# Prologue of a two-layer encoder kernel: squares on other engines, one transposition earlier, three small loads on ScalarE's queue

## The chip, the cores and the metric

The kernel runs on one core of one Trainium2 chip. The metric is the device time of one execution in microseconds; three runs of the kernel before gave 933.13, 933.24 and 934.04 us, and their median, 933.24 us, is the time before. A core has a tensor engine (TensorE, PE in the profile; its weight loads are PEld), a vector engine (VectorE, DVE), a scalar engine (ScalarE, ACT), GpSimd (POOL) and SyncE (SP), which here only starts transfers. Transfers (DMAs) can be started from the queues of SyncE, ScalarE and GpSimd.

## The reference

A trunk of two layers works on 512 tokens of 1024 numbers, all float32. Layer 0 mixes by dilated window attention (three dilations, 8 heads of 128), layer 1 by grouped-query attention with rotary angles over a grid; both also attend to 256 memory tokens with 4 heads. Cut to what matters here:

```python
for i in range(DEPTH):                       # 2 layers
    h = rmsnorm(x, norm_g[i])                # x * rsqrt(mean(x*x) + EPS) * g
    mem_h = rmsnorm(mem, mem_norm_g[i])
    proj = einsum('bsd,de->bse', h, w_in)    # q, k, v of the mixer, memory queries, gate
    o_mix = mixer(...)                       # q and k normed per head (qn, kn), rotary, softmax, values
    o_mem = memory_attention(q_mem, mem_h, w_mem_kv[i], ...)
    y = concat([o_mix, o_mem]) * silu(gate)
    x = x + einsum('bse,ed->bsd', y, w_out[i])
```

The squares in this text are the `mean(x*x)` of the first two lines for layer 0. The "table" is the rotary table of layer 0 (`tab_a`), the "norm rows" are `qn_a` and `kn_a`, the first 32 gains of each.

## The kernel before

**Products.** Every float32 matmul is made of three: an operand is cut into a high part (a cast to the matmul type, on ScalarE) and a low part (what is left, a subtraction on VectorE). A matmul group computes high x high and low(activation) x high(weight) first (`mm_early`, L178 and L179), then high(activation) x low(weight) (`mm_late`, L182). Large products are done by a seven-product scheme over quarter matrices (`s_chunk`); the memory keys and values of layer 0 are plain products (`proj_t` through `chunk`).

**Weights.** `Weights` loads tiles `wl` of 512 KB by SyncE's queue (L260), adds some of them up (L291 on VectorE, L287 to L306 as adding transfers from GpSimd's queue), casts them to `wh` on ScalarE (L331, with a gain; L333) and subtracts to `wo` on VectorE (L345, L347). `advance` does this once for each group of matmuls: low parts, sums, high parts, loads.

**Order of the work.** The order on each engine is the order in which the Python program emits instructions. `Driver` keeps it: after each group of 8 early and 4 late matmuls comes a `tick`, a slot; generators that were spawned with a delay take a step when their slot has come, in the order in which they were spawned, and `yield n` asks for n slots. An engine works in order, so an instruction that waits holds up everything behind it on that engine. Each of the three DMA queues is in order in the same way.

**The prologue.** Slots 1 to 8 are the memory keys and values (two products of two halves `u` of the weights, each with two blocks `b` of 128 memory tokens); slots 9 to 22 are the first seven products of layer 0 on the tokens. Before the first group, SyncE issues the memory rows (`mt`, in four pieces of 256 KB), the first weights, four blocks of tokens (`xt`, 512 KB each) and the gains, interleaved. Then, line by line:

- `square(b, j)` (L1276 on ScalarE, L1278 on VectorE) takes the squares of a piece of memory rows; `factor(b)` makes from them the root of the mean on GpSimd (L1283, `rstd_of` L535 and L536).
- `place_m(b, j)` (L1288) transposes a piece on TensorE (`turn4`, L589: four transposes into one bank) and cuts it into high and low (`split`, L166 on ScalarE, L169 on VectorE). `place_m(1, 0)` makes the first half of block 1, the operand of the second group.
- `ahead(u, b)` (L1311) is what is put between the early and the late matmuls of the groups of the memory keys; `proj_t` (L606) calls it as `mid`. In slot 1, `(0, 0)`, that is: square of piece (1, 0) on ScalarE, `place_m(1, 0)`, square of piece (0, 1) on VectorE, and two high weight parts (L331).
- `norm_1(xb, both)` (L568) takes the squares of a token block: both halves on ScalarE (L576) for `both` 0, the second half on VectorE (L574) for 1, both halves on VectorE for 2; then three small GpSimd instructions (L578, L535, L536) make the root. `norm_2` (L583) scales the block by it on VectorE.
- `prep` (L1223) is the generator for the token blocks. Its slots 4, 5, 6 are `c` = 2, 3, 4. In slot 4 it takes the squares of blocks 2 and 3 (of block 2 one half on ScalarE and one on VectorE, of block 3 both on VectorE) and brings in block 0 (`first_t`, L644: eight transposes L589, two casts L166, two subtractions L169, two copies L650). In slot 5 it scales block 2 and brings in block 1; in slot 6 it scales block 3. From slot 7 on (`diffs_t`, `rest_t`) the sums and differences of the blocks are made.
- The evacuation of the memory keys (`ev_k`, L764) squares them per head on ScalarE (`head_sq`, L704, four instructions) and makes its root on GpSimd (L535, L536 with four columns, then L770).
- `setup` (L1253) is spawned for slot `SET_AT` = 15: it issues three loads on SyncE's queue, the rotary table (128 rows of 1024 bytes) and twice 3 x 32 gains to all 128 partitions (384 pieces of 128 bytes each), and four slots later (slot 19) begins the small computations with them on VectorE (L1259 to L1263), later the table itself (L1266).

```python
    drv.spawn(prep(), PD)            # PD = 2
    drv.spawn(setup(), SET_AT)       # 15
    ...
    km, vm = mem_kv(0, M, ahead)     # slots 1 to 8
    s_chunk(512, H, ev_v0, tight=True)   # slots 9 to 22
```

Of the kernel before, what the change touches and what calls it, by code (L numbers as in the profile page):

```python
# [21 lines left out]
TCKW = {}  # L22
NBIG, NM4, NS2, SCRATCH = 7, 23, 14, 2048
RING, LEAD = 4, 2
BULK, ACTIVE, SET_AT, MEM_B, PREP_Y, PREP_B, HALF, SET_B = 2, 2, 15, 14, 1, 1, {"a": 3, "b": 3, "o": 0}, 12
MEM_STEP = 1, 1
MEM_D = 4
PAUSE = 2
# [105 lines left out]
def trunk_kernel(ctx: ExitStack, tc: tile.TileContext, x, mem, wall, norm_g, mem_norm_g, gcol,  # L134
                 qn_a, kn_a, qn_b, kn_b, ident_d, mask_d, tab_a, tab_b, out):
    nc = tc.nc
# [15 lines left out]
    def s2(dt=F32, name="s2"):  # L152
        return pool.tile([128, 512], dt, tag="s2", name=name, bufs=NS2)
# [7 lines left out]
    def sm(n, name):  # L161
        return small.tile([128, n], F32, tag="sm%d" % n, name=name)
# [13 lines left out]
    def mm_early(o, a, b, c, d, start):  # L176

        T.matmul(o, a, b, start=start, stop=False, skip_group_check=True)  # L178
        T.matmul(o, c, d, start=False, stop=False, skip_group_check=True)  # L179

    def mm_late(o, a, b, stop):
        T.matmul(o, a, b, start=False, stop=stop, skip_group_check=True)  # L182
# [200 lines left out]
    def chunk(units, nb, group, evac):  # L383

        ps = [None] * nb
        for u in range(units):
            w = []
            for h, l in (W.take(), W.take()):
                w += [(h[:, k * 512:(k + 1) * 512], l[:, k * 512:(k + 1) * 512]) for k in range(2)]
            for b in range(nb):  # L390
                if u == 0:
                    ps[b] = pj()
                group(w, u, b, ps[b])
                drv.free()
                if u == units - 1:
                    drv.release(evac(b, ps[b]), 2)
                W.advance()
                drv.tick()
# [132 lines left out]
    def rstd_of(ss, n):  # L531

        r = sm(n, "rstd")
        e = sm(n, "mse")
        G.tensor_scalar(e, ss, EPS, None, ALU.add)  # L535
        G.tensor_tensor(r, e, half[:, 0:n], ALU.pow)  # L536
        return r
# [30 lines left out]
    def norm_1(xb, both=False):  # L568

        ss = sm(2, "ss")  # L570
        for j in range(2):
            jk = s2(name="sq")
            if both and (j or both == 2):
                V.tensor_tensor_reduce(jk, xb[j], xb[j], 1.0 / 1024.0, 0.0, ALU.mult, ALU.add, ss[:, j:j + 1])  # L574
            else:
                A.activation(jk, xb[j], AF.Square, scale=1.0 / 32.0, accum_out=ss[:, j:j + 1])  # L576
        r, e = sm(1, "rstd"), sm(1, "mse")
        G.tensor_tensor(e, ss[:, 0:1], ss[:, 1:2], ALU.add)  # L578
        return rstd_of(e, 1)

    def norm_2(xb, r, row, js=(0, 1)):
        for j in js:
            V.scalar_tensor_tensor(xb[j], xb[j], r, row[j], ALU.mult, ALU.mult)  # L583
# [22 lines left out]
    def proj_t(act, sels, evac, mid=None):  # L606

        def group(w, u, b, p):
            for k in range(4):
                kk = 4 * u + k  # L610
                mm_early(p, sels[b](act, 0, kk), w[k][0], sels[b](act, 1, kk), w[k][0], kk == 0)
            if mid:
                mid(u, b)
            for k in range(4):
                kk = 4 * u + k
                mm_late(p, sels[b](act, 0, kk), w[k][1], kk == 7)
        chunk(2, len(sels), group, evac)
# [26 lines left out]
    def first_t(H, top, c, view=same, turn=same):  # L644

        ps = [(k, turn(turn4(top[j], None, None)), [view(t) for t in slot(H, k, c)]) for k, j in (("12", 1), ("11", 0))]
        for k, p, hl in ps:
            split(*hl, p)
        for k, p, _ in ps:
            A.copy(view(whole(k, c)), p)  # L650

    def diffs_t(H, low, c, view=same, turn=same, late=False):

        f22 = whole("22", c)
        A.copy(view(f22), turn(turn4(low[1], None, None)))
        p = turn(turn4(low[0], None, None))
        yield 1
        s1, s3 = whole("S1", c), whole("S3", c)
        V.tensor_tensor(view(s1), p, view(f22), ALU.subtract)
        V.tensor_tensor(view(s3), view(full["11", c]), p, ALU.subtract)  # L660
        hl = slot(H, "S1", c)
        if late:
            drv.late(lambda: split(*hl, s1))
        else:
            split(*hl, s1)

    def rest_t(H, c, ds, spread=False):

        def put(k, f):
            hi, lo = slot(H, k, c)  # L670
            A.copy(hi, f)

            def low():
                V.tensor_tensor(lo, f, hi.bitcast(F32), ALU.subtract)
                yield 1

            if c and k == "S2" and not spread:
                drv.release(low(), 1)
            else:
                (drv.soon if spread and c and k == "S2" else drv.late)(lambda: next(low()))  # L680

        s1, s2_, s4, s3, f22 = [full.pop((k, c)) for k in ("S1", "11", "12", "S3", "22")]
        V.tensor_tensor(s2_, s1, s2_, ALU.subtract)
        if not spread:
            V.tensor_tensor(s4, s4, s2_, ALU.add)
        put("S2", s2_)
        if spread:
            yield ds[0] - 1
            V.tensor_tensor(s4, s4, s2_, ALU.add)
            yield 1  # L690
        else:
            yield ds[0]
        put("S4", s4)
        yield ds[1]
        put("S3", s3)
        yield ds[2]
        put("22", f22)
        yield 1
# [24 lines left out]
    def halves(t):  # L723
        return [t[:, 0:512], t[:, 512:1024]]
# [483 lines left out]
    tabA = s2(name="tabA")[:, 0:256].rearrange("p (b c d) -> p b c d", b=2, c=4)  # L1208
    grA = s2(name="grA")[:, 0:192].rearrange("p (s c) -> p s c", s=6)
# [9 lines left out]
    xb = [halves(t) for t in xt]  # L1219

    n = {}

    def prep():  # L1223

        for c in range(5):
            if c > 2:
                norm_2(xb[c - 1], n[c - 1], rows["x"])
            if c == 2:
                n[2], n[3] = norm_1(xb[2], 1), norm_1(xb[3], 2)
            if 1 < c < 4:  # L1230
                first_t(H, xb[c - 2], c - 2, by_class, from_rows)
            yield 1

        def forms(c):
            yield from diffs_t(H, xb[2 + c], c, by_class, from_rows, late=True)
            yield 3
            yield from rest_t(H, c, (2, 2, 2))

        drv.spawn(forms(1), 1)
        yield from forms(0)  # L1240
# [11 lines left out]

    def setup():  # L1253

        nc.sync.dma_start(tabA.rearrange("p b c d -> p (b c d)"), tab_a.rearrange("(a i) f -> i a f", i=4))
        nc.sync.dma_start(grA[:, 0:3], qn_a[0:1, :, 0:32].to_broadcast([128, 3, 32]))
        nc.sync.dma_start(grA[:, 3:6], kn_a[0:1, :, 0:32].to_broadcast([128, 3, 32]))
        yield 4
        V.tensor_tensor(gk, gc[:, 0:3], gc[:, 3:6], ALU.mult)  # L1259
        V.tensor_scalar(gk, gk, QS, None, ALU.mult)  # L1260
        V.tensor_scalar(gc[:, 6:8], gc[:, 6:8], QS, None, ALU.mult)
        V.memset(gk[0:32, :], 1.0)
        V.tensor_scalar(grA[:, 0:3], grA[:, 0:3], QS, None, ALU.mult)  # L1263
        yield 6
        for cs_ in range(2):
            V.tensor_tensor(ropeA[:, cs_], tabA[:, cs_, :, None, :].to_broadcast([128, 4, 6, 32]),  # L1266
                            grA[:, None].to_broadcast([128, 4, 6, 32]), ALU.mult)
            yield 1
# [4 lines left out]
    def square(b, j, act=True):  # L1273

        if act:
            A.activation(s2(name="sq"), mb[b][j], AF.Square, scale=1.0 / 32.0, accum_out=ss[b][:, j:j + 1])  # L1276
        else:
            V.tensor_tensor_reduce(s2(name="sq"), mb[b][j], mb[b][j], 1.0 / 1024.0, 0.0, ALU.mult, ALU.add, ss[b][:, j:j + 1])  # L1278
# [9 lines left out]
    def place_m(b, j, act=True):  # L1288

        p = turn4(mb[b][j], None, None)  # L1290
        split(*[M.block(n, j, slice(b * 128, (b + 1) * 128)) for n in range(2)], p, act)
# [19 lines left out]
    def ahead(u, b):  # L1311

        if (u, b) == (0, 0):
            square(1, 0)
            place_m(1, 0)
            square(0, 1, False)
            W.hi(True)
            W.hi(True)
        if (u, b) == (0, 1):
            place_m(0, 1)  # L1320
            factor(0)
            square(1, 1, False)
            place_m(1, 1)
            n[0] = norm_1(xb[0])
            n[1] = norm_1(xb[1])
            factor(1)
        if (u, b) == (1, 0):
            norm_2(xb[0], n[0], rows["x"])
            norm_2(xb[1], n[1], rows["x"])
# [660 lines left out]
```

## Time and profile before

| | |
|---|---|
| median of three runs | 933.24 us (933.13 to 934.04) |
| profiled execution, its own time | 933.17 us |
| span of its profile, first to last instruction | 931.4 us |
| TensorE busy | 924.8 us, 99% |
| weight loads of TensorE | 814.7 us, 87% |
| VectorE busy | 801.7 us, 86% |
| ScalarE busy | 695.7 us, 75% |
| GpSimd busy | 360.5 us, 39% |
| granted TensorE clock | 1.000 |

Rows of the timeline read: start in us, duration in us, engine, line, operation, output <- inputs, shapes, how many in a row; in brackets the time for which the engine stood before it and what ended that. A `q` behind an engine's name means its instruction sequencer, where DMAs are issued. Rows of the waits read: who waited, for whom, us in total, times, longest. Rows of the stretches read: from:to, length, then busy us and number of instructions for PE, PEld, DVE, ACT, POOL, then the granted clock, the busy share of the DMA engines and GB/s. Rows of the chain read: start, duration, what. A line number names the line of the kernel before, and of a helper where a helper emits the instruction.

### The profile page before, as it was taken

The numbers are of one execution on the slowest core, as the hardware profiler recorded it, in microseconds if no ns is written. First come the engines' busy times: TensorE is split into PE (matmuls) and PEld (weight loads), VectorE is DVE, ScalarE is ACT, GpSimd is POOL, SyncE is SP. The second block draws the span as 40 slices with busy tenths as digits, with TensorE's granted clock in tenths as the row PEclk, the third lists the DMA queues.
The fourth block names the chain that finished last, engine by engine and source line by source line (L and its number), as shares of the span: only waits on it lengthen the run. The fifth ranks groups of instructions, "written<-read, shape, count | busy, mean of one in ns | idle before, by whom it ended". The sixth has DMA issues, their size and how long they took to land.

```text
span 931.4 us, 16276 instructions
## 1 busy us (share of the span) xinstructions
PE 924.8 (99%) x5471; PEld 814.7 (87%) x5471; DVE 801.7 (86%) x1457; ACT 695.7 (75%) x1725; POOL 360.5 (39%) x504
## 2 busy tenths in 40 slices
PE   9999999999999999999999999999999999999998
PEld 7789888888888888888889998888988999999886
DVE  6999677879888888979798989999898998789977
ACT  7775789677868686867776767757879887789774
POOL 4411425556564646464746102234252440110122
PEclk9999999999999999999999999999999999999999
DMA  9999948968686778686867899999985687785777
GB/s 351 389 264 331 300 127 218 319 146 247 162 248 166 249 160 271 159 272 135 241 178 207 231 261 271 289 320 331 289 219 114 178 233 178 201 227 116 200 162 181
DMA packets 83179, 212.85 MB, mean 229 GB/s; under 512 B 18960, under 2 KB 25752, under 8 KB 83096
## 3 DMA queue, kind: packets, MB, share of 16 engines
q1 hardware_dynamic: 60744, 141.16, 42.3%
q0 software_dynamic: 20384, 67.12, 39.1%
q10 hardware_dynamic: 1968, 3.54, 1.0%
q8 instruction: 43, 0.70, 0.3%
q14 instruction: 40, 0.33, 0.1%
HBM read 162.96 MB, written 12.65 MB: 189 GB/s over the span
## 4 chain that ended last, share of the span: by engine, by line
PE 91%; DVE 5%; DMA 2%; ACT 1%; SPq 0%; issue 0%; DVEq 0%; ACTq 0%
PE pj L178 24%; PE pj L179 24%; PE pj L182 24%; PE qT L716 3%; PE sa L1476 2%; PE oo L1585 2%; PE ptb L1819 1%; PE sa L1472 1%; DVE wo L347 1%; PE pt L1564 1%; DMA x<-in_x_dram 1%; DMA row<-in_norm_g_dram 1%; PE ob L178 1%; PE ob L182 1%; PE ob L179 1%; PE xT L589 1%
## 5 line engine op out<-in xcount | busy, mean ns | idle before, releaser
L347 DVE TENSOR_TENSOR wo<-wl,wh 128x1024 fp32r<-128x1024 f32 x253 | 308.8, 1225 | 5.6 <-ACT wh L333 5.6
L333 ACT CAST wh<-wl 128x1024 fp32r<-128x1024 f32 x253 | 267.3, 1061 | 27.5 <-PE pj L179 19.5
L178 PE MATMUL pj<-wh,hS 128*128 128x512 f32 (+1 forms) x416 | 154.5, 380 | 0.0
L179 PE MATMUL pj<-wh,hS 128*128 128x512 f32 (+1 forms) x416 | 148.9, 367 | 0.0
L178 PE MATMUL pj<-wh,h 128*128 128x512 f32 (+1 forms) x312 | 115.3, 378 | 0.0
L179 PE MATMUL pj<-wh,h 128*128 128x512 f32 (+1 forms) x312 | 111.6, 367 | 0.0
L536 POOL TENSOR_TENSOR rstd<-mse,half 128x4 f32<-128x4 f32 (+2 forms) x98 | 102.0, 1041 | 8.2
L182 PE MATMUL pj<-wo,hS 128*128 128x512 f32 (+1 forms) x416 | 99.5, 366 | 0.0
L179 PEld LDWEIGHTS pj<-wh,hS 128*128 128x128 f32 x416 | 78.7, 189 | 11.2
L178 PEld LDWEIGHTS pj<-wh,hS 128*128 128x128 f32 x416 | 78.6, 189 | 11.0
L535 POOL TENSOR_SCALAR mse<-hss 128x4 f32<-128x4 f32 (+1 forms) x88 | 45.6, 519 | 104.4 <-ACT junk L704 91.3
L182 PEld LDWEIGHTS pj<-wo,hS 128*128 128x128 f32 x416 | 72.4, 189 | 13.0 <-DVE wo L347 0.2
L704 ACT ACTIVATE junk<-sn 128x128 f32<-128x128 f32 x264 | 79.3, 310 | 3.4 <-DVE sn L428 3.4
L260 POOL DMA_DIRECT2D wl<-in_wall_dram x44 | 41.9, 982 | 95.4 <-DMA wl<-in_wall_dram 21.7
L1417 POOL TENSOR_TENSOR ta<-sn,tabs 128x128 f32<-128x128 f32 (+1 forms) x64 | 38.3, 605 | 104.0 <-DVE sn L709 80.4
L415 ACT COPY sn<-pj 128x512 f32<-128x512 f32 x122 | 67.2, 590 | 12.3 <-PE pj L182 12.3
L182 PE MATMUL pj<-wo,h 128*128 128x512 f32 (+1 forms) x312 | 74.5, 366 | 0.0
L306 POOL DMA_DIRECT2D wl<-wl x35 | 31.0, 895 | 109.2 <-DVE wo L347 48.7
L438 DVE TENSOR_TENSOR sn<-pj,sn 128x512 f32<-128x512 f32 x89 | 60.7, 683 | 6.5 <-PE pj L182 6.2
L179 PEld LDWEIGHTS pj<-wh,h 128*128 128x128 f32 x312 | 59.0, 189 | 8.4
L178 PEld LDWEIGHTS pj<-wh,h 128*128 128x128 f32 x312 | 59.0, 189 | 8.2
L296 POOL DMA_DIRECT2D wl<-wl x35 | 32.9, 964 | 78.7 <-DVE wl L291 18.9
(299 smaller groups left out, 2403.0 us busy)
## 6 DMA issues: line engine op xcount, KB each, us to landing
wl<-in_wall_dram SPq DMA_DIRECT2D x226, 512.0 KB, 7.4
wl<-wl POOLq DMA_DIRECT2D x70, 512.0 KB, 5.9
wl<-in_wall_dram POOLq DMA_DIRECT2D x48, 512.0 KB, 8.6
od<-o SPq DMA_DIRECT2D x9, 256.0 KB, 5.8
x<-in_x_dram SPq DMA_DIRECT2D x4, 512.0 KB
v0r<-sn SPq DMA_DIRECT2D x8, 256.0 KB, 8.5
v0d<-v0r SPq DMA_DIRECT2D x4, 512.0 KB
og<-od ACTq DMA_DIRECT2D x4, 512.0 KB
```

What stands on the lines that cost most here:

```text
L178: T.matmul(o, a, b, start=start, stop=False, skip_group_check=True)
L179: T.matmul(o, c, d, start=False, stop=False, skip_group_check=True)
L182: T.matmul(o, a, b, start=False, stop=stop, skip_group_check=True)
L260: queue.dma_start(t, wall[d], **how)
L333: A.copy(wh, self.tile[key])
L347: V.tensor_tensor(wo, self.tile[key], wh.bitcast(F32), ALU.subtract)
L415: A.copy(t_, b_)
L438: V.tensor_tensor(t_, b_, t_, ALU.subtract if q == "12" and late is None else ALU.add)
L535: G.tensor_scalar(e, ss, EPS, None, ALU.add)
L536: G.tensor_tensor(r, e, half[:, 0:n], ALU.pow)
L704: A.activation(jk, p[:, j * 128:(j + 1) * 128], AF.Square, scale=by, accum_out=ss[:, j:j + 1])
L1417: G.tensor_tensor(ta[:, 0:n], xn[:, 0:n, 0:32], ropeA[:, 0, b, s0:s0 + n], ALU.mult)
```

## The change

Four edits, all in what is emitted for the first 20 slots:

- In `proj_t`, `mid` is called inside the loop over the early matmuls. For the group `(0, 0)` it comes after the second of the four pairs, for the others after the fourth, as before.
- In `ahead` for `(0, 0)`, `place_m(1, 0)` is emitted ahead of the square of piece (1, 0); both use ScalarE.
- In `prep`, the squares of block 2 are taken in slot 4 with both halves on VectorE, and those of block 3 in slot 5 with both halves on ScalarE, behind the scaling of block 2 and ahead of `first_t` of block 1.
- In `setup`, the three loads are issued by ScalarE's queue, and in slot 12 (`SET_AT` 12); the wait behind them is 7 slots, so that the computation begins in slot 19 as before.

```diff
-BULK, ACTIVE, SET_AT, MEM_B, PREP_Y, PREP_B, HALF, SET_B = 2, 2, 15, 14, 1, 1, {"a": 3, "b": 3, "o": 0}, 12
+BULK, ACTIVE, SET_AT, MEM_B, PREP_Y, PREP_B, HALF, SET_B = 2, 2, 12, 14, 1, 1, {"a": 3, "b": 3, "o": 0}, 12
@@ proj_t
                 mm_early(p, sels[b](act, 0, kk), w[k][0], sels[b](act, 1, kk), w[k][0], kk == 0)
-            if mid:
-                mid(u, b)
+                if mid and k == (1 if (u, b) == (0, 0) else 3):
+                    mid(u, b)
@@ prep
-            if c == 2:
-                n[2], n[3] = norm_1(xb[2], 1), norm_1(xb[3], 2)
+            if 1 < c < 4:
+                n[c] = norm_1(xb[c], 2 * (c == 2))
             if 1 < c < 4:
                 first_t(H, xb[c - 2], c - 2, by_class, from_rows)
@@ setup
-        nc.sync.dma_start(tabA.rearrange("p b c d -> p (b c d)"), tab_a.rearrange("(a i) f -> i a f", i=4))
-        nc.sync.dma_start(grA[:, 0:3], qn_a[0:1, :, 0:32].to_broadcast([128, 3, 32]))
-        nc.sync.dma_start(grA[:, 3:6], kn_a[0:1, :, 0:32].to_broadcast([128, 3, 32]))
-        yield 4
+        nc.scalar.dma_start(tabA.rearrange("p b c d -> p (b c d)"), tab_a.rearrange("(a i) f -> i a f", i=4))
+        nc.scalar.dma_start(grA[:, 0:3], qn_a[0:1, :, 0:32].to_broadcast([128, 3, 32]))
+        nc.scalar.dma_start(grA[:, 3:6], kn_a[0:1, :, 0:32].to_broadcast([128, 3, 32]))
+        yield 7
@@ ahead
         if (u, b) == (0, 0):
+            place_m(1, 0)
             square(1, 0)
-            place_m(1, 0)
             square(0, 1, False)
```

## Prediction

> **What bounds the kernel now.** I read the page's busy times, then who waited for whom on TensorE, then the chain that ended last, then each engine's timeline over the first 60 us.
>
> ```profile
> span 931.4 us, 16276 instructions
> PE 924.8 (99%) x5471; PEld 814.7 (87%) x5471; DVE 801.7 (86%) x1457; ACT 695.7 (75%) x1725; POOL 360.5 (39%) x504
> ```
>
> ```profile
> PE xT L589 <- DVE x L583: 1.0, 1, 1.0
> PEld pj L182 <- DVE wo L347: 0.2, 1, 0.2
> ```
>
> TensorE is busy 924.8 of 931.4 us. The first row below the busy times is the longest of its waits once the kernel has begun, and the second one is the kind on which the argument ends. All of this change lies before 60 us. So the only question is how much earlier TensorE can run when it leaves the start of the kernel; whatever stays lost or won there is lost or won at the end, since nothing later waits.
>
> ```profile
> 14.78 10.06 DMA x<-in_x_dram
> 30.00:35.00 5.00, 3.97 (x22) 3.14 (x21) 5.00 (x9) 3.37 (x6) 2.13 (x4) 1.00 1.03 409
> 31.64 1.06 PE L589 MATMUL xT<-ident,x 128*128 128x128 f32 x8 [1.03 <-DVE x L583]
> ```
>
> The chain goes back over the load of the fourth token block, which lands at 14.78 + 10.06 = 24.84. From 30 to 35 us TensorE loses the 1.03 us of the third row, while VectorE (DVE) is busy 5.00 of 5.00 and the DMA engines are full (share 1.03, 409 GB/s). So the landings are fixed, and VectorE's order of work decides.
>
> **The squares: where the gain should come from.** These rows are VectorE's, then ScalarE's (ACT).
>
> ```profile
> 23.07 0.69 DVE L574 CUSTOM_DVE_ANT_0 sq<-x 128x512 f32<-128x512 f32 x1
> 24.86 0.69 DVE L574 CUSTOM_DVE_ANT_0 sq<-x 128x512 f32<-128x512 f32 x1 [1.10 <-DMA x<-in_x_dram]
> 25.48 0.69 DVE L574 CUSTOM_DVE_ANT_0 sq<-x 128x512 f32<-128x512 f32 x1
> 26.12 1.29 DVE L169 TENSOR_TENSOR h<-xT,h 128x512 fp32r<-128x512 f32 x2
> 27.33 2.73 DVE L345 SCALAR_TENSOR_TENSOR wo<-wl,gmc,wh 128x512 fp32r<-128x512 f32 x4
> 29.97 1.41 DVE L583 SCALAR_TENSOR_TENSOR x<-x,rstd,row 128x512 f32<-128x512 f32 x2
> 31.30 1.28 DVE L169 TENSOR_TENSOR h<-xT,h 128x512 fp32r<-128x512 f32 x2
> 32.50 1.41 DVE L583 SCALAR_TENSOR_TENSOR x<-x,rstd,row 128x512 f32<-128x512 f32 x2
> ```
>
> ```profile
> 22.38 2.62 ACT L331 ACTIVATE wh<-wl,gmc 128x512 fp32r<-128x512 f32 x4 [0.96 <-DMA wl<-in_wall_dram]
> 24.91 0.62 ACT L576 ACTIVATE sq<-x 128x512 f32<-128x512 f32 x1
> 25.52 1.05 ACT L166 CAST h<-xT 128x512 fp32r<-128x512 f32 x2
> 29.30 1.09 ACT L166 CAST h<-xT 128x512 fp32r<-128x512 f32 x2
> ```
>
> Before, VectorE squares one half of block 2 and both of block 3, and stands 1.10 us in front of block 3's load. After, it squares both halves of block 2, at 23.07 and 23.68, and is free at 24.3. ScalarE no longer squares at 24.91, so its cast there starts at 24.91 instead of 25.52; it can't be earlier, as the four weight casts in front wait for a landing. VectorE's subtraction at 26.12, which needs the first cast, then starts at 25.52 - 0.61 + 0.6 = 25.51: 0.61 earlier. What follows on it is back to back, so the weights go from 27.33 to 26.72 and the scaling of block 2 from 29.97 to 29.36. TensorE's transposes that waited start at 31.03, not 31.64. So far: 0.61 won. The 1.10 us that VectorE stood and 0.61 of a square (1.7 us) shrink to this because ScalarE is late next.
>
> ScalarE now squares both halves of block 3 a slot later, 2 x 0.61 = 1.22 us, ahead of the casts at 29.30. These come at 29.30 - 0.61 + 1.22 = 29.91 and end by 31.0; VectorE's subtraction wants them from 30.69 and 31.3, so that is covered, with 0.2 to 0.3 us to spare.
>
> The second price is on GpSimd (POOL), which makes the root of the mean square of block 3 in three instructions.
>
> ```profile
> 15.70 0.19 POOL L578 TENSOR_TENSOR mse<-ss 128x1 f32<-128x1 f32 x1 [0.90 <-ACT sq L576]
> 16.29 0.58 POOL L536 TENSOR_TENSOR rstd<-mse,half 128x1 f32<-128x1 f32 x1
> 27.16 0.20 POOL L578 TENSOR_TENSOR mse<-ss 128x1 f32<-128x1 f32 x1
> 28.23 0.93 POOL L536 TENSOR_TENSOR rstd<-mse,half 128x1 f32<-128x1 f32 x1
> 30.23 1.39 POOL L536 TENSOR_TENSOR rstd<-mse,half 128x4 f32<-128x4 f32 x1
> ```
>
> Before, the trio ran from 27.16 to 29.16, long before its user at 32.50. Now it stands in order behind the key's root (30.23 to 31.62, 0.61 earlier: to 31.01), while the squares end at 29.9 already. The first and last of three rows give the trio 1.17 us (15.70 to 16.87) or 2.00 (27.16 to 29.16). It was slow while VectorE worked on weights and fast while VectorE stood. In its new place VectorE is at the end of a subtraction and then idle, so I take 1.3. Ready: 31.01 + 0.1 + 1.3 = 32.4, by the two ends 32.3 to 33.1. So the scaling at 32.50 moves by -0.2 to +0.6; I take -0.1. Here the 0.61 is given back.
>
> **Where VectorE's place is passed on to TensorE.**
>
> ```profile
> 45.00:50.00 5.00, 5.00 (x23) 4.14 (x23) 4.61 (x7) 4.67 (x7) 2.75 (x4) 1.00 1.06 290
> 53.52 1.22 DVE L347 TENSOR_TENSOR wo<-wl,wh 128x1024 fp32r<-128x1024 f32 x1
> 54.82 1.16 PE L182 MATMUL pj<-wo,hS 128*128 128x512 f32 x4
> 51.11 0.62 ACT L671 CAST hS<-f 128x512 fp32r<-128x512 f32 x1 [1.39 <-DVE f L683]
> 52.92 0.68 DVE L674 TENSOR_TENSOR hS<-f,hS 128x512 fp32r<-128x512 f32 x1
> ```
>
> From 32.50 on VectorE has little idle time (its least busy 5 us up to 55 are the first row's, 4.61 of 5.00, and what it waits for there, ScalarE's casts, follows from its own results) until it ends a low weight part at 53.52 + 1.22 = 54.74, and TensorE takes it at 54.82 (the 0.2 us wait on L347 above is of this kind). The slack is 0.08 us. If TensorE comes 0.61 earlier it stands here until VectorE is done. So the end moves by what VectorE's row at 32.50 moves: -0.1 us, not -0.61. If VectorE comes 0.6 later, TensorE loses that.
>
> **The moved transposition.**
>
> ```profile
> 7.72 0.50 PE L178 MATMUL pj<-wh,act 128*128 128x512 f32 x1
> 8.91 0.60 PE L589 MATMUL xT<-ident,m 128*128 128x128 f32 x4
> 10.91 0.50 PE L179 MATMUL pj<-wh,act 128*128 128x512 f32 x1 [0.23 <-DVE act L169]
> 8.37 0.63 ACT L1276 ACTIVATE sq<-m 128x512 f32<-128x512 f32 x1
> SPq L260 <- DMA m<-in_mem_dram: 1.1, 1, 1.1
> ```
>
> The four transposes go ahead of the four matmuls of the first group that begin at 7.72. SyncE's wait for the memory rows (last row: its queue's waits from 7.5 to 9 us) ends about when ScalarE's square of the same rows starts, at 8.37; I read this as their landing. So the transposes start 8.91 - 8.37 = 0.54 earlier and no more, and four matmuls whose operands are there stand behind them. These took at most 8.91 - 7.72 = 1.19 us, so the group ends up to 1.19 - 0.54 = 0.65 later. In return ScalarE's cast of the transposed rows goes ahead of its 0.63 us square, and the matmul at 10.91, which waits for these rows, gains up to 0.63. The two about cancel. I count this at nothing because TensorE stands at 31.64 anyhow: it came there at 31.64 - 1.03 = 30.61, and the new start is 31.03, so 0.4 us of loss or any gain disappears there. Without that cover it would cost at most the 0.65.
>
> **The three loads.**
>
> ```profile
> 53.97 0.72 SPq L1255 DMA_DIRECT2D tabA<-in_tab_a_dram  x1
> 54.80 0.58 SPq L1256 DMA_DIRECT2D grA<-in_qn_a_dram  x1
> 55.43 4.72 SPq L1257 DMA_DIRECT2D grA<-in_kn_a_dram  x1
> 60.20 5.86 SPq L260 DMA_DIRECT2D wl<-in_wall_dram  x5
> 511.32 0.41 ACTq L895 DMA_DIRECT2D og<-od  x1
> 511.77 0.51 ACTq L895 DMA_DIRECT2D og<-od  x1
> ```
>
> SyncE loses three issues, 0.72 + 0.58 + 4.72 = 6.0 us, and the weight loads behind them start about 6 us earlier. TensorE waits for none of these, so that is worth 0. ScalarE's queue gets them in slot 12, just ahead of the cast at 51.11, where ScalarE stands 1.39 us, from 49.72 on. Their price there: 0.41 to 0.51 each on ScalarE's own rows, or with SyncE's durations 0.72 + 2 x 0.58 = 1.9. I take 1.9: from 49.72 they end at 51.6, 0.5 late for the cast at 51.11, which then ends at 52.2. What is queued behind them on ScalarE is that cast, and VectorE's L674 at 52.92 wants it: in time with 0.7 us to spare. Price 0, by that cover. Their computation stays in its slot (12 + 7 = 15 + 4).
>
> The Trainium skill ("DMA: Bandwidth & Descriptors", section "Issuing engines are not separate DMA queues") says that starting DMAs from several engines saves only the sequencer's time to start them, usually little beside the transfer. The row of 4.72 us is not little here. By the page SyncE gains next to nothing, by the row 6 us, and the end moves by 0 in either case.
>
> **Sum.** Profiled execution 933.17 us (span 931.4, 1.8 around it); the median of the runs shown is 933.24. Squares -0.1, transposition 0, loads 0: 933.1. The runs shown spread over 0.9 us, so I take 0.2% (1.9 us) as what a measurement can tell from no change.
>
> **Rivals.** (B) GpSimd's trio takes the slow 2.0 us; VectorE stands for it at 32.0 and starts the scaling 0.6 later than before. Slower by 0.6: 933.9. For it: 27.16 to 29.16; against it: VectorE idles beside the trio. Chance 0.22. (C) On the other side and beyond what can be told: ScalarE's queue is held at an issue as SyncE's was. 0.72 + 0.58 + 4.72 from 49.72 on ends at 55.7; the cast ends at 56.4, VectorE's L674 starts there in place of 52.92, and the low weight part and TensorE follow 3.4 later: 936.5. It decides once the three issues take over 52.92 - 0.62 - 49.72 = 2.6 us together. For it: it is the same load that took SyncE 4.72. Against it: the one just before it, of the same size, took 0.58, and ScalarE's queue has nothing else in front. Chance 0.08. (D) The root is ready in time and VectorE keeps its 0.61: 932.6. It needs the trio in under 1.0 us or an earlier key root. Chance 0.2. (E) The edit does nothing where it says, as the memory rows land too late for the transposes: this changes only what 31.64 hides, and is in the forecast, 0.46.
>
> **Numbers.** Forecast 933.1. The range runs from (D) less half the spread of the runs, 932.1, to (B) by its end plus the same, 934.4; only (C) is outside. No case gives 1.9 us faster: the named waits that the change can reach are less. For what I don't see I keep 0.04, of which 0.03 faster and 0.01 slower. So faster 0.03, slower 0.08 + 0.01 = 0.09, no change 0.46 + 0.22 + 0.2 = 0.88.
>
> **What would show it.** After: transposes of block 2 at about 31.0; the wait of 1.10 on the load gone from VectorE, and a new one of some tenths on GpSimd's root ahead of L583; TensorE waiting 0.3 to 0.6 us for wo at about 54.7; no ScalarE issue of the three over 0.8 us. It is wrong if TensorE passes 54.8 by more than a half us earlier without standing, if VectorE has real idle time between 33 and 54 us that I took for work, or if ScalarE stands at an issue.

## The result, and the profile after

The change made the kernel slower: 941.09 us, the median of 6 runs (937.84 to 941.82), against 933.64 for the kernel before (6 runs beside it, 933.01 to 934.95). The ratio (of the means, so not quite that of the two medians) is 1.0072, with a 95% interval of 1.0054 to 1.0089. The forecast was 933.1 and its range ended at 934.4. (Two runs of 1142 and 1312 us, one of a variant below and one of the kernel before, had a granted clock of 0.75 and 0.66 over the whole run, and are left out of what follows.)

The profiled execution took 940.84 us with a span of 939.1, 7.7 more than before. First the page, then TensorE's longest waits once the kernel has begun.

```profile
span 939.1 us, 16277 instructions
PE 927.1 (99%) x5471; PEld 816.5 (87%) x5471; DVE 801.5 (85%) x1455; ACT 696.7 (74%) x1727; POOL 359.9 (38%) x504
```

```profile
PE pj L178 <- DVE sn L438: 5.6, 1, 5.6
PE xT L589 <- ACT h L166: 0.8, 1, 0.8
```

The 1.0 us at block 2's transposes has become 0.8, and there is one new wait of 5.6 us. The chain of waits says whose it is (start, length, what).

```profile
48.81 25.59 DMA grA<-in_qn_a_dram
...
74.43 0.04 DVE grA L1263
...
75.16 0.69 DVE sn L438
75.85 0.14 issue
75.99 0.77 PE pj L178
```

The chain goes through one of the three moved loads. Issued on ScalarE's queue at 48.81, it lands at 48.81 + 25.59 = 74.40. VectorE's timeline shows what that does, first before, then after.

```profile
68.93 0.20 DVE L1263 TENSOR_SCALAR grA<-grA 128x96 f32<-128x96 f32 x1
```

```profile
68.60 0.06 DVE L1262 MEMSET gk<- 32x3 f32 x1
74.43 0.21 DVE L1263 TENSOR_SCALAR grA<-grA 128x96 f32<-128x96 f32 x1 [5.77 <-DMA grA<-in_qn_a_dram]
74.56 0.68 DVE L790 TENSOR_TENSOR vm<-vr,vm 128x512 fp32r<-128x512 f32 x1
75.16 0.68 DVE L438 TENSOR_TENSOR sn<-pj,sn 128x512 f32<-128x512 f32 x1
```

Before, the scaling of the norm rows (0.2 us of work) found its rows there and nothing marks a wait. After, VectorE stands 5.77 us in front of it, and the evacuation L438, queued two places behind, is what frees the PSUM bank (one of the pieces of the memory that TensorE writes to) that TensorE wants. TensorE then runs slowly for a while. In this table by stage (busy time of each engine in each stretch) the third number from the right is the granted clock.

```profile
68.00:72.00 4.00, 2.36 (x11) 1.63 (x9) 0.62 (x5) 2.02 (x3) 0.00 (x0) 1.00 1.04 268
72.00:76.00 4.00, 0.01 (x1) 0.04 (x1) 1.57 (x4) 0.00 (x0) 0.00 (x0) 0.78 0.45 115
76.00:80.00 4.00, 4.00 (x10) 3.13 (x11) 4.00 (x5) 1.04 (x1) 0.88 (x1) 0.50 0.76 244
80.00:84.00 4.00, 4.00 (x21) 3.45 (x20) 2.36 (x4) 1.05 (x1) 0.00 (x1) 0.87 1.02 362
84.00:88.00 4.00, 4.00 (x35) 4.00 (x35) 4.00 (x5) 1.55 (x3) 0.87 (x1) 1.00 1.04 299
```

From 76 to 80 the clock is 0.50. In the chain the matmuls follow each other there at 0.43 us and not 0.23, until 81.1. Matched one by one with the kernel before, TensorE's matmuls start 0.60 us *earlier* up to 69.3 (after's time), 5.19 us later at 75.99, and 7.67 us later when the clock is back; from there to the end the difference stays within 0.2. So 5.19 + 0.60 = 5.8 us are the stand, 7.67 - 5.19 = 2.5 the half clock, and 0.6 had been won: 5.8 + 2.5 - 0.6 = 7.7, the whole of it.

The issues themselves, which the prediction had costed, were as cheap as it said:

```profile
48.06 0.66 ACTq L1255 DMA_DIRECT2D tabA<-in_tab_a_dram  x1
48.81 0.52 ACTq L1256 DMA_DIRECT2D grA<-in_qn_a_dram  x1
49.38 0.58 ACTq L1257 DMA_DIRECT2D grA<-in_kn_a_dram  x1
50.51 0.62 ACT L671 CAST hS<-f 128x512 fp32r<-128x512 f32 x1 [1.42 <-DVE f L683]
```

ScalarE still stands 1.42 us in front of its cast. The cost is not in issuing but in landing. And it has a second victim, SyncE's queue, which from 46 to 80 us waits for these loads:

```profile
SPq L260 <- DMA tabA<-in_tab_a_dram: 11.0, 1, 11.0
SPq L260 <- DMA grA<-in_qn_a_dram: 8.7, 1, 8.7
52.85 22.96 SPq L260 DMA_DIRECT2D wl<-in_wall_dram  x6
```

In the program as built, the loads of SyncE and ScalarE take eight completion semaphores (counters that a landing load raises) in turn, and each load waits until the one before it on its semaphore has landed. So a weight load on SyncE waits for the table on ScalarE. The last row has the six weight loads of that stretch: the sixth went out at 75.48, and before at 65.74.

Why does it take so long? Packets counted from the trace of after, per stretch of 2 us, by queue (GpSimd's accumulating loads in 4096-byte packets, SyncE's, and ScalarE's three loads):

```
us       GpSimd  SyncE  ScalarE
54..56     94      27     94
56..58     91      85     90
58..60     86      88     87
60..62     81      84     84
66..68     75      58     27
68..70     85      66     27
```

While all three queues have work, each gets the same number of packets: the DMA engines take the queues in turn, packet by packet, and a piece of 128 bytes waits for its turn behind 4096-byte packets (about 0.33 us each on GpSimd's queue, 0.16 on SyncE's) like any other. From 66 on only few engines still have pieces. The completion increments show which: twelve of the sixteen engines end the first norm rows by 61.6, the last four at 71.2, 73.5, 73.9 and 74.4, and the table too is counted by four engines alone, from 64.4 to 65.3. The table's load has 4 as its outermost dimension, so it rides on four engines, ahead of the norm rows there.

The Trainium skill ("DMA: Bandwidth & Descriptors") states both: engines go round the queues that have work, packet by packet ("Queues, rings and completion order"), and a load is split over the largest number of engines up to 16 that divides the slowest dimension of both of its sides ("Why a DMA increments its semaphore by 16 and not by 1"). The counts above agree with the first, the four increments with the second.

### The profile page after: what moved, and what is told of

The parts are those of the page before. It is cut to its first block, busy times and chain, and to the rows that moved or that the text cites. A ratio compares the mean times of both kernels' runs of the same rounds, so it can differ in the third digit from the quotient of the medians.

```text
span 939.1 us, 16277 instructions
## 1 busy us (share of the span) xinstructions
PE 927.1 (99%) x5471; PEld 816.5 (87%) x5471; DVE 801.5 (85%) x1455; ACT 696.7 (74%) x1727; POOL 359.9 (38%) x504
## 4 chain that ended last, share of the span: by engine, by line
PE 86%; DVE 6%; DMA 5%; ACT 2%; issue 1%; SPq 0%; POOL 0%; DVEq 0%; ACTq 0%
PE pj L178 23%; PE pj L179 23%; PE pj L182 23%; DMA grA<-in_qn_a_dram 3%; PE qT L716 2%; DVE wo L347 2%; PE sa L1476 2%; PE oo L1585 2%; PE ptb L1819 1%; PE sa L1472 1%; PE pt L1564 1%; DMA wl<-in_wall_dram 1%; PE ob L178 1%; PE ob L182 1%; PE ob L179 1%; DMA m<-in_mem_dram 1%
## 5 line engine op out<-in xcount | busy, mean ns | idle before, releaser
L536 POOL TENSOR_TENSOR rstd<-mse,half 128x4 f32<-128x4 f32 (+2 forms) x98 | 102.4, 1045 | 8.2
L535 POOL TENSOR_SCALAR mse<-hss 128x4 f32<-128x4 f32 (+1 forms) x88 | 45.1, 512 | 113.9 <-ACT junk L704 101.0
L260 POOL DMA_DIRECT2D wl<-in_wall_dram x44 | 41.9, 981 | 91.2 <-DMA wl<-in_wall_dram 24.0
L306 POOL DMA_DIRECT2D wl<-wl x35 | 31.4, 905 | 113.8 <-DVE wo L347 54.9
L438 DVE TENSOR_TENSOR sn<-pj,sn 128x512 f32<-128x512 f32 x89 | 60.9, 685 | 8.6 <-PE pj L182 8.3
L182 PEld LDWEIGHTS pj<-wo,h 128*128 128x128 f32 x312 | 54.9, 191 | 10.0
```

Of the source, the lines that this page charges most:

```text
L260: queue.dma_start(t, wall[d], **how)
L438: V.tensor_tensor(t_, b_, t_, ALU.subtract if q == "12" and late is None else ALU.add)
```

## The experiments

**Theory 1:** the late landing of the first norm rows on ScalarE's queue holds VectorE, and through it TensorE. **Theory 2:** SyncE, held for the same landings, brings weights late. **Theory 3:** it was the squares or the transposition. Times are medians, each beside runs of the kernel before on the same chip: 933.70 (22 runs) for the first four, 933.93 (23) for the next four, 933.67 (33) for the last four.

**The loads alone.** The kernel before with

```diff
-BULK, ACTIVE, SET_AT, ... = 2, 2, 15, ...
+BULK, ACTIVE, SET_AT, ... = 2, 2, 12, ...
-        nc.sync.dma_start(tabA...   (and both grA loads)
-        yield 4
+        nc.scalar.dma_start(tabA...
+        yield 7
```

> The kernel before with nothing but the three loads moved: ScalarE's queue, slot 12, computation 7 slots later. Theory 1 (the first grA load lands some 25 us after its issue, at about 74, and VectorE stands for it at the scaling of grA with its later work queued behind): the landing sets the end of the stand, whatever TensorE had won before, so the time is that of the kernel after, 940 to 942, with the same stand on VectorE, some 5 us long. Theory 2 (SyncE's queue, held for the same landings, brings the weights late): the same time; the other runs tell it from theory 1. Theory 3 (the squares or the transposition cost it): 933.6 +- 0.5, no stand on grA.

938.2 us, ratio 1.0054 (1.0041 to 1.0066). The stand on VectorE is the same, 5.76 us up to 74.72. But TensorE lost only 4.4 us: it did sixteen more matmuls first and then stood for a weight part.

```profile
PE pj L182 <- DVE wo L347: 3.0, 1, 3.0
```

So theory 1 or 2 holds for the larger part, and about 3 us of the 7.5 need the other edits as well. The built programs tell why. The projections' tiles rotate over four banks, and with the squares moved the rotation changes:

```
before               4 7 6 5 4 6 7 5 4 6 4 7 6 5 4 6
loads alone          4 7 6 5 4 6 7 5 4 6 4 7 6 5 4 6
transposition alone  4 7 6 5 4 6 7 5 4 6 4 7 6 5 4 6
squares alone        4 7 6 5 4 6 7 5 4 6 4 6 7 5 4 6
after                4 7 6 5 4 6 7 5 4 6 4 6 7 5 4 6
```

With the squares in, the matmul at 70.79 (before's time) has a wait for VectorE's evacuation L438 in the program, which it doesn't have without them. Every run below that has the squares and a late VectorE shows this wait; this one shows none. The bank order was not changed by itself.

**Everything but the loads.** The kernel after with the loads on SyncE's queue, `SET_AT` 15 and `yield 4`, as before.

> The kernel after with the three loads back on SyncE's queue in slot 15; squares and transposition as in after. Theories 1 and 2: no stand on grA; TensorE keeps what it won by 70 us, 0.64 us: 932.5 to 933.1. Theory 3: 940 to 942.

933.33 us, ratio 1.0001 (0.9990 to 1.0013); 11 of 12 runs lie from 933.04 to 933.70, so theory 3 falls: the squares and the transposition cost nothing by themselves. The twelfth, the profiled one, took 939.45: there the first norm rows landed at 72.46 and VectorE stood 3.7 us for them. So even on SyncE's queue the landing is a race. Before it is 66.33 against 68.93; in the other profiled runs below with the same issue in slot 15 on SyncE's queue it is 66.80, 67.26 and 69.97.

**Norm rows first.** The kernel after with the table's load behind the two others:

```diff
-        nc.scalar.dma_start(tabA...
         nc.scalar.dma_start(grA[:, 0:3]...
         nc.scalar.dma_start(grA[:, 3:6]...
+        nc.scalar.dma_start(tabA...
```

> The kernel after with only the order of the three issues on ScalarE's queue changed: the two grA loads ahead of tabA. tabA's packets ride on few of the DMA engines; behind the grA rows they no longer stand in front of them. Theory 1: the first grA load lands at 57 to 62, before VectorE wants it at 68.4; no stand; 932.5 to 934. tabA still lands at about 74, long before its use at about 83. Theory 2: SyncE still waits for tabA until about 74, the weights come as late as in after, TensorE stands 4 us or more: 938 or more. Theory 3: 940 to 942.

935.15 us, ratio 1.0020 (1.0011 to 1.0029). The rows landed 12.7 us after their issue, at 60.77, as theory 1 says; VectorE's scaling is at 69.29 without a wait.

```profile
69.29 0.20 DVE L1263 TENSOR_SCALAR grA<-grA 128x96 f32<-128x96 f32 x1
```

Of the 7.5 us 6 are gone, but not all. What is left comes by theory 2, as far as the waits show it: SyncE waited 8.8 us for the table and 6.5 and 6.4 for the norm rows, so that its sixth weight load went out at 77.00 (before at 65.74); VectorE stood 0.8 for a weight (L291); GpSimd's issue L260, which waits for a weight's landing, came 1.9 us later than before, and with it the root queued behind it (L535, L536), which TensorE's transposes at 101 us want.

```profile
PE qT L1381 <- DVE sn L709: 1.0, 1, 1.0
PE pj L178 <- DVE sn L438: 0.3, 1, 0.3
```

**Use them later.** The kernel after with the scaling of the norm rows put behind the `yield 6`, in front of the product with the table.

> The kernel after with VectorE's scaling of grA put 6 slots later, in front of the product with the table; all loads as in after. The loads land as late as in after (74 to 75). Theory 1: VectorE doesn't stand, TensorE doesn't either: 932.5 to 934. Theory 2: SyncE's weight loads are as late as in after, so TensorE stands for weights: 938 or more. Theory 3: 940 to 942.

936.02 us, ratio 1.0031 (1.0019 to 1.0043). The rows land at 75.23 and nobody minds. But SyncE waits 11.3 and 8.9 us for table and rows, and the price appears elsewhere:

```profile
81.00 1.23 DVE L291 TENSOR_TENSOR wl<-wl 128x1024 f32<-128x1024 f32 x1 [3.80 <-DMA wl<-in_wall_dram]
```

```profile
PE pj L178 <- DVE sn L438: 1.8, 1, 1.8
PE qT L1381 <- DVE sn L709: 0.7, 1, 0.7
```

Both theories are right: theory 1 for most of it, theory 2 for 1.5 to 2.3 us. This share is read from the waits of these two runs; no run takes away SyncE's hold and nothing else. In the kernel after no such wait shows behind 76 us: its longer stand covers it.

**ScalarE's queue, old slot.** The kernel after with `SET_AT` 15 and `yield 4`, loads still on ScalarE's queue.

> The kernel after with the three loads still on ScalarE's queue, but issued in slot 15 as before (4 slots ahead of the computation). Theory 1 (the DMA engines take the queues in turn, packet by packet, so the loads' small packets go out at one per round with GpSimd's and SyncE's 4096-byte packets): 56 packets of tabA and the first grA rows on the busiest engines at 0.40 to 0.44 us each, as in after, from about 53.5 on: landing at 76 to 78, VectorE stands 8 to 10 us, TensorE 2 to 4 us longer than in after: 943 to 945. Rival (slot 12 is at fault, because it meets more of the accumulating traffic; ScalarE's queue is as good as SyncE's): landing at about 66, as before, 932.5 to 934.

943.41 us, ratio 1.0102 (1.0089 to 1.0115). The rows land at 76.94, issued at 53.39:

```profile
76.97 0.21 DVE L1263 TENSOR_SCALAR grA<-grA 128x96 f32<-128x96 f32 x1 [8.13 <-DMA grA<-in_qn_a_dram]
```

Landing and time are as theory 1 had worked out from packets and rounds. The earlier slot helped; the queue is what hurts.

**SyncE's queue, new slot.** The kernel after with `nc.sync` for the three loads, `SET_AT` 12 and `yield 7` kept.

> The kernel after with the three loads on SyncE's queue in slot 12 (7 slots ahead of the computation): the slot of after, the queue of before. Theory 1: on SyncE's queue the small packets share each engine only with the accumulating queue until 62 and then run at 0.05 us each; they land at 63 to 67, no stand at the scaling of grA: 932.5 to 934.5. Rival (the slot is at fault): landing at about 74, 940 to 942.

937.46 us, ratio 1.0039 (1.0026 to 1.0052). The rows landed at 64.09 and VectorE didn't stand for them, as expected; the time was not. In one queue what is issued behind the loads is behind them on the engines too:

```profile
ACT sn L415 <- DMA v0r<-sn: 3.2, 1, 3.2
```

```profile
DVE h L674 <- ACT h L671: 3.1, 1, 3.1
```

```profile
PE pj L178 <- DVE sn L438: 2.6, 2, 2.3
```

ScalarE waits for a store of `sn` that followed the loads on SyncE's queue, VectorE for ScalarE's cast, TensorE for VectorE. So neither rival of that run was right, and a free landing isn't all that counts.

**The table in four loads.** The kernel after with

```diff
-        nc.scalar.dma_start(tabA...("p b c d -> p (b c d)"), tab_a.rearrange("(a i) f -> i a f", i=4))
+        for i in range(4):
+            nc.scalar.dma_start(tabA...("p b c d -> p (b c d)")[32 * i:32 * i + 32], tab_a.rearrange("(a i) f -> i a f", i=4)[i])
```

> The kernel after with the table loaded in four loads of 32 rows each, so that it rides on all DMA engines and not on four; queue, slot and order stay. Theory 1: 8 + 24 packets stand on every engine up to the end of the first grA rows, in place of 32 + 24 on four of them: at 0.36 to 0.44 us they land at 62 to 66, ahead of VectorE's use at 68.4; no stand there. The second grA rows land at 67 to 70, and SyncE's queue is held for them as long: 932.5 to 935. Rival (the bytes or the count of small packets as a whole set the landing): 72 to 75, 939 to 942.

934.38 us, ratio 1.0006 (0.9997 to 1.0015). All sixteen engines count for each piece; the table is there at 56.94, the first norm rows at 67.05 (a little after the 62 to 66 expected), no stand. The same bytes and the same 768 small pieces, so the rival falls: the four overloaded engines set the landing. The second rows came only at 76.1, and six issues on ScalarE make its casts late (VectorE waits 1.3 us for them), which costs TensorE about 1 us up to 55 us.

**The squares alone**, on the kernel before (`prep` as in the diff):

> The kernel before with the squares of blocks 2 and 3 moved alone. By the prediction's sum (0.61 won at 31.64 and given back at the low weight part): -0.1, 933.1 against 933.2. By what the trace after shows up to 70 us (VectorE keeps it): -0.3 to -0.6. Rival: the order of the projection banks that this edit also changes makes TensorE wait for VectorE's eviction near 70: 0 to +0.5.

933.64 us (11 runs), ratio 1.0006 (0.9992 to 1.0020): no difference that this can tell. In the profiled run (933.0) TensorE ends 0.13 us earlier, the -0.1 of the sum. But two of the others took 937.5 and 939.8 (and two more 935.8 and 935.9), where none of the 78 runs of the kernel before beside these experiments is above 935.9. With the new bank order a late landing costs at once; that this is what held those runs is not shown, as only the run of 933.0 has a trace.

**GpSimd's queue.** The kernel after with `nc.gpsimd` for the three loads.

> The kernel after with the three loads on GpSimd's queue, slot 12. They no longer use the eight semaphores that SyncE's and ScalarE's loads take in turn, so SyncE's weight loads can't be held for them; and they follow the accumulating packets in one queue in place of taking turns with them. Theory 1 (small packets wait for their turn): landing by about 62, no stand at the scaling of grA. Theory 2 (SyncE's hold brought the weights late): SyncE stands for no landing of tabA or grA. Price on the other side: GpSimd issues two accumulating loads 3 to 4 us later. 933 to 936. If it is 938 or more with no stand on grA, the late accumulating loads are dearer than I take them.

934.9 us, ratio 1.0011 (1.0002 to 1.0020). The last column of this row of the list of DMA issues is the time from issue to landing:

```profile
grA<-in_qn_a_dram POOLq DMA_DIRECT2D x1, 48.0 KB, 7.8
```

7.8 us in place of 25.6, from the same slot, and SyncE waits for none of the three. The small pieces follow the 4096-byte packets in one queue and are then served one after the other. What remains is the price named, though larger: GpSimd's two adding transfers (L306) are issued 6.8 and 4.4 us later than before, ScalarE's casts wait for the first of them, VectorE for the casts, and TensorE stands 1.3 us behind VectorE.

**Back on SyncE, used late.** The version without the loads' move and with the late scaling:

> The kernel after with the three loads back on SyncE's queue in slot 15, and VectorE's scaling of grA 6 slots later, in front of the product with the table. If the odd run of 939 of the kernel with the loads put back (its landing was at 72.5) is a late landing of grA, it can't come here: 932.5 to 933.5 in all runs, none over 935. Rival (the odd runs have another cause): runs of 935 to 940 remain.

933.41 us (932.86 to 934.49, 11 runs), ratio 0.9997 (0.9988 to 1.0006). No odd runs are left, which speaks for the late landing as their cause, though with one odd run in twelve eleven even ones could also be chance. TensorE has its 0.54 us gain at 54.8 and loses it at 101:

```profile
101.43 0.66 PE L1381 MATMUL qT<-ident,sn 128*128 128x128 f32 x4 [0.40 <-DVE sn L709]
```

```profile
97.09 0.93 POOL L260 DMA_DIRECT2D wl<-in_wall_dram  x1 [8.22 <-DMA wl<-in_wall_dram]
```

GpSimd's root for these transposes stands behind this issue, which waits for a weight's landing (96.35 before). TensorE had come 0.52 us earlier than before; this issue came 0.7 later.

**The transposition alone**, on the kernel before:

> The kernel before with the transposition of the memory rows moved ahead in the first group, alone. By the prediction: 0 at the end, since TensorE stands about 1 us at 31.64 anyhow: 933.0 to 933.9, within 0.2 of before. Rival: its gain reaches VectorE through the memory keys' earlier matmuls, and 0.2 to 0.4 is kept: 932.7 to 933.0.

933.29 us, ratio 0.9997 (0.9988 to 1.0006). TensorE is 0.44 us early at 15 us and 0.10 at 30.0, and 0.14 late at the end: nothing is kept, as predicted. In this run the first norm rows landed at 69.97, VectorE stood 0.9 us for them and ended L438 at 71.4. The matmul that waits for L438 in the new bank order started at 70.7 without a stand: with the old order a late VectorE costs TensorE nothing here.

**All three remedies:** SyncE's queue, slot 15, late scaling, table in four loads.

> As the version with the loads back on SyncE and the late scaling, and the table in four loads of 32 rows, which ride on all DMA engines: the small packets end earlier (8 + 24 + 24 an engine in place of up to 80), so that SyncE's weight loads behind them start earlier too. 932.5 to 933.3; rival (three more issues of 0.4 to 0.7 us on SyncE delay the weights): 933.5 to 935.

933.55 us (932.56 to 934.24), ratio 0.9996 (0.9987 to 1.0005). No version beats the kernel before by more than can be told.

## Why the prediction was wrong

**The step that failed** is the three loads: "Price 0, by that cover" and "Their computation stays in its slot (12 + 7 = 15 + 4)". It costed the issues on both queues and the engine that issues, and nowhere asked when the loads land. It took for granted that a load issued 6 us earlier lands earlier. Measured: 54.80 to 66.33 on SyncE's queue, 48.81 to 74.41 on ScalarE's, against a use at 68.7. That is 4.4 us when the loads move alone, and 7.5 with the rest.

Rows for it were within reach: the landing before had only 68.93 - 66.33 = 2.6 us to spare, the DMA engines were full from 45 to 50 us, and the prediction itself held that SyncE's queue would bring its weight loads 6 us earlier, which compete with the small loads.

**What SyncE gains:** "worth 0" was too good. It got rid of a 4.72 us issue and stood 11.0 and 8.7 us for landings in its place, through the shared semaphores. That is 1.5 to 2.3 us where nothing longer covers it.

**ScalarE's issues:** right, 0.66, 0.52 and 0.58 us, below the 0.8 named. Rival (C), the one on the slow side, had the sign but not the mechanism: no issue was held.

**The squares:** VectorE's stand of 1.10 us went, and in its place VectorE stands 1.04 us for ScalarE's cast, the limit that the prediction named. The transposes of block 2 start at 30.72, 0.92 us earlier. 0.61 of this came as worked out; 0.29 more are a weight's landing, which the prediction held fixed. ScalarE's four casts behind it start at 22.09 and not at 22.38:

```profile
22.09 2.61 ACT L331 ACTIVATE wh<-wl,gmc 128x512 fp32r<-128x512 f32 x4 [0.88 <-DMA wl<-in_wall_dram]
```

The next step, "Here the 0.61 is given back", was mis-sized:

```profile
30.66 0.20 POOL L578 TENSOR_TENSOR mse<-ss 128x1 f32<-128x1 f32 x1
30.95 0.22 POOL L535 TENSOR_SCALAR mse<-mse 128x1 f32<-128x1 f32 x1
31.26 0.57 POOL L536 TENSOR_TENSOR rstd<-mse,half 128x1 f32<-128x1 f32 x1
```

```profile
31.87 1.43 DVE L583 SCALAR_TENSOR_TENSOR x<-x,rstd,row 128x512 f32<-128x512 f32 x2 [0.20 <-POOL rstd L536]
```

```profile
54.19 1.20 PE L182 MATMUL pj<-wo,hS 128*128 128x512 f32 x4
```

GpSimd's trio took its fast 1.17 us and began at once behind the key's root, where the sum had 1.3 and a gap of 0.1. So VectorE's scaling came 0.63 earlier (32.50 to 31.87), and TensorE at 54.82 also 0.63 (54.19). But 0.29 of this is the landing again: in the nine profiled runs with the new squares in which these four casts run in one row, the scaling starts 9.76 to 9.79 us behind their start, and in the three with the old squares 10.07 to 10.12. The squares are thus worth about 0.3 us there: more than the 0.1 of the sum, and half of the 0.61 that rival (D) keeps.

Up to 55 us the way was the one written: what VectorE's scaling moves, TensorE moves behind the low weight part, 0.63 in the kernel after and 0.17 in the profiled run of the squares alone, where the weights landed later. That this run ended 0.13 earlier, so near the -0.1 of the sum, is in part the luck of that landing. "Nothing later waits" was wrong twice: at 70, where VectorE's stand is passed on, and at 101, where the gain runs into a landing.

**The transposition:** "0.54 earlier and no more" rested on one landing of the memory rows. The transposes wait for it, and in the profiled runs with this edit they start between 7.96 (after, 0.95 earlier than before) and 8.87, with TensorE 0.6 early to 0.4 late at 20 us. Alone nothing of its gain is kept, as the sum had it.

## What to carry to other kernels

When a load moves to another queue, work out its landing and not only its issue: count its pieces on the busiest DMA engine, and multiply by a round over all queues with work, since a 128-byte piece waits as long for its turn as a 4096-byte packet. Then ask who is queued behind the first use, and which queue shares its completion semaphores. And where an early part runs faster, look for the next landing that the gain will run into before it is counted at the end.

## What was not expected of the hardware

A stand of TensorE costs more than its length. After stands of 3.0 us (the loads alone), 3.5 (everything but the loads), 5.6 (after) and 8.1 (ScalarE's queue, old slot) the granted clock fell to 0.50 and the matmuls' spacing doubled, which added 1.4, 3.0, 2.5 and 2.9 us; after 2.3 us (SyncE's queue, new slot) it stayed at 1.00. In these four traces the clock fell 2.4, 2.9, 3.9 and 3.8 us after the stand had begun and was half for 3.4, 6.8, 6.8 and 10.2 us, that is for one, two, two and three times 3.4 us. The Trainium skill ("TensorE: Matmul & The Clock Gate", "Part 1: The HAM clock gate") has the clock halved by an idle window of about 3.4 us, which these rows bear out roughly; but here 3.0 us was enough once, and the half clock lasted 5 us beyond the first matmul (75.99 to 81.1).

One issue before took 4.72 us on SyncE's queue, with 128-byte pieces in it; the same issue on ScalarE's queue took 0.58, and the load that was quicker to issue was slower to land.
